# MLP of a hybrid decoder layer: first matrix in quarters 2 to 4 as seven half products a block, accumulations by ScalarE and adding transfers

## The chip, the cores and the metric

The kernel runs on one core of a Trainium2 chip. The metric is the device time of one execution in microseconds (us). Engines are named as the profile names them: PE is TensorE, PEld its weight loads, DVE is VectorE, ACT is ScalarE, POOL is GpSimd, SP is the engine whose queue starts most transfers. PSUM is the memory that PE writes to: here it is eight banks of 512 float32 columns on 128 partitions. All matrices are float32. The kernel keeps each operand as a high part rounded to PE's fp32r format and a low part that holds the rest, and makes a product from three matmuls (high by high, high by low, low by high).

## The reference

A decoder layer of 512 tokens and width 1024: two mixing branches and an output projection, then the MLP, then a gated embedding and a final norm. The change lies in the MLP:

```python
u = rmsnorm(x, norm_mlp_g[i]) @ w_up[i]              # 512 x 1024 by 1024 x 4096
x = x + jnp.square(jax.nn.relu(u)) @ w_down[i]       # 512 x 4096 by 4096 x 1024
```

The row factor of the norm commutes with the rest: relu(r a) squared is r squared times relu(a) squared. So the kernel applies only the gain ahead of the first matrix, and multiplies by the squared row factor (`r2`) when the products of the second matrix are added to x.

## The kernel before, in words

The MLP works through the 4096 hidden features in four quarters of 1024 (`for q in range(4)` near the end of `block_kernel`): `up(q)` computes a quarter's features with the first matrix, `down(q)` multiplies them by the second matrix and adds to `xk`, four tiles of 128 tokens by 1024 columns.

The input of the first matrix, `x1`, is held turned: eight tiles of 128 channels by 512 tokens, in two parts. `up` (L1239) makes eight tiles of 128 features, each a chain (`mm_T`) of 8 x 3 matmuls with the weights stationary and 512 tokens moving, into one of two banks (`ps_g`). ACT takes relu and square (L1248, L1252) into a feature tile `F`. The first two of quarter 1 are made ahead by `begin_up` (L1188), between the transposes of x1.

`down` (L1269) uses the Strassen-Winograd scheme: the two operands are cut into 2 x 2 blocks, and seven products of half size on sums and differences of blocks (named A11, A12, A22 for a block itself, S1 to S4 for sums) take the place of eight. Each product is two halves of the contraction (`kh`), two halves of the tokens (`t`) and 2 x 3 matmuls with 512 moving columns: 7 x 24 = 168 matmuls a quarter. The feature sums are made by DVE in `F` (L1262 to L1265) and split into two parts, the weight sums by DVE in place in the loaded tiles (L1302, L1306, L1320, L1326). Products accumulate in three pairs of banks X, Y, Z. `acc` (L1286) has DVE scale each half by `r2` and add it to `xk`, twelve times a quarter. The first product is part of all four output blocks: it is copied or added to a tile `p1` in each quarter, and after the last quarter scaled and added to the three blocks that don't hold it already, by six adding transfers that POOL starts (`acc_p1`, L1293).

Each weight tile of 128 x 1024 is loaded by SP into a raw tile (`wr`, four slots, or `wd`, six slots), and split by `load_w` (L156) into `wh` (ACT cast, L137) and `wl` (DVE subtraction, L138). There are four buffers of each (`WB`, L30), so splits run a few products ahead of PE and no further.

The framework sorts each engine's instructions into one fixed order when the program is built, by readiness and by their place in the text, and adds the semaphore waits. At run time each engine takes its own list in order; an instruction that waits holds those behind it. SP's loads and POOL's transfers are such lists too.

## Time and profile before

| | us |
|---|---|
| median of three runs | 870.41 (870.24 to 871.0) |
| the profiled execution | 870.98 |
| its span, first to last instruction | 869.0 |
| PE, DVE, ACT, POOL busy in the span | 859.4, 664.2, 496.6, 51.0 |

The span is what the profile covers; the time of the same execution is 1.98 us longer. A profile row gives the line of the kernel, the engine, the operation, what it writes and reads with shapes, the count, the busy time, the mean duration in ns of one, and the engine's idle time ahead with what ended it. Matmuls overlap each other, so the mean of one matmul is longer than the step from one to the next; the chain of waits and its counts give the step.

### The profile page before, as it was taken

To read this page: it belongs to the slowest core of one execution; us is meant where nothing else is said; L and a number is where in the kernel's file an instruction comes from. 1 tells how busy PE (TensorE), PEld (TensorE's weight loads), DVE (VectorE), ACT (ScalarE), POOL (GpSimd) and SP (SyncE) were. 2 spreads that over 40 slices of the span, in tenths; PEclk is the share of its full clock that TensorE was granted. 3 is DMA by queue.
4 is the path that set the end of the run, shared out by engine and by line. 5 is a ranking of instruction groups with operands and counts; after the bars stand their busy time and mean duration, and the time that the engine had idled before them with its cause. 6 is when DMAs were issued, how large, how long until landed. Compare 5 with 4: busy or idle time off the path is not lost.

```text
span 869.0 us, 11746 instructions
## 1 busy us (share of the span) xinstructions
PE 859.4 (99%) x4422; PEld 725.1 (83%) x4422; DVE 664.2 (76%) x978; ACT 496.6 (57%) x845; POOL 51.0 (6%) x81
## 2 busy tenths in 40 slices
PE   9999999999999999999999999999999999999996
PEld 7888789999877868888888888888888888888886
DVE  6898978774698898767896669746965795688657
ACT  6776657554676677854344565345535533564743
POOL 2221111000000000000020000000000000002000
PEclk9999999999999999999999999999999999999999
DMA  8677235436121256565244611630252044206502
GB/s 282 212 184 294 93 126 195 165 127 218 50 97 47 76 197 244 194 250 181 74 74 145 242 49 49 202 113 25 82 209 97 1 146 170 73 25 137 178 1 97
DMA packets 36234, 117.76 MB, mean 136 GB/s; under 512 B 5069, under 2 KB 5069, under 8 KB 36178
## 3 DMA queue, kind: packets, MB, share of 16 engines
q1 hardware_dynamic: 28578, 95.77, 31.6%
q0 software_dynamic: 7456, 20.98, 8.8%
q8 instruction: 34, 0.56, 0.3%
q10 hardware_dynamic: 144, 0.26, 0.1%
q14 instruction: 22, 0.18, 0.1%
HBM read 99.17 MB, written 11.54 MB: 127 GB/s over the span
## 4 chain that ended last, share of the span: by engine, by line
PE 86%; issue 7%; DVE 3%; ACT 2%; DMA 1%; SPq 0%; POOL 0%; POOLq 0%; ACTq 0%; DVEq 0%
PE psg L176 44%; PE psp L176 23%; PE psa L176 10%; PE pst L176 4%; PE psp L1121 1%; DMA xt<-in_x 1%; PE pst L853 1%; PE psa L783 1%; PE psa L784 1%; ACT wh L137 0%; DVE wl L138 0%; ACT lm L808 0%; DMA wh<-in_w_b 0%; PE psa L933 0%; PE psa L953 0%
## 5 line engine op out<-in xcount | busy, mean ns | idle before, releaser
L137 ACT CAST wh<-wr 128x1024 fp32r<-128x1024 f32 x129 | 135.8, 1053 | 157.0 <-PE psg L176 60.8
L138 DVE TENSOR_TENSOR wl<-wr,wh 128x1024 fp32r<-128x1024 f32 x129 | 157.2, 1220 | 81.8 <-ACT wh L137 81.5
L176 PE MATMUL psg<-x,wh 128*128 128x512 f32 x512 | 157.7, 389 | 0.0
L176 PE MATMUL psp<-wh,uf 128*128 128x512 f32 x448 | 138.5, 389 | 0.0
L176 PEld LDWEIGHTS psg<-x,wh 128*128 128x128 f32 x512 | 96.0, 188 | 20.0
L176 PE MATMUL psg<-x,wl 128*128 128x512 f32 x256 | 99.6, 389 | 0.0
L176 PEld LDWEIGHTS psp<-wh,uf 128*128 128x128 f32 x448 | 84.1, 188 | 17.4
L176 PE MATMUL psp<-wl,uf 128*128 128x512 f32 x224 | 87.1, 389 | 0.0
L176 PE MATMUL psg<-h,wh 128*128 128x512 f32 x256 | 80.1, 393 | 0.0
L137 ACT CAST wh<-wd 128x1024 fp32r<-128x1024 f32 x44 | 46.2, 1053 | 54.1 <-PE psp L176 21.9
L138 DVE TENSOR_TENSOR wl<-wd,wh 128x1024 fp32r<-128x1024 f32 x44 | 53.2, 1220 | 14.6 <-ACT wh L137 14.5
L176 PEld LDWEIGHTS psg<-x,wl 128*128 128x128 f32 x256 | 48.0, 188 | 9.9
L176 PEld LDWEIGHTS psg<-h,wh 128*128 128x128 f32 x256 | 46.9, 188 | 8.8
L176 PE MATMUL psg<-h,wl 128*128 128x512 f32 x128 | 50.0, 391 | 0.0
L138 DVE TENSOR_TENSOR uf<-F,uf 128x1792 fp32r<-128x1792 f32 (+2 forms) x20 | 33.0, 1652 | 21.8 <-ACT uf L137 21.8
L176 PEld LDWEIGHTS psp<-wl,uf 128*128 128x128 f32 x224 | 42.0, 188 | 8.9
L176 PE MATMUL psg<-yb,wh 128*128 128x512 f32 x128 | 40.1, 393 | 0.0
L1289 DVE SCALAR_TENSOR_TENSOR xk<-psp,r,xk 128x512 f32<-128x512 f32 x48 | 33.8, 745 | 8.0 <-PE psp L176 7.7
L137 ACT CAST uf<-F 128x1792 fp32r<-128x1792 f32 (+2 forms) x20 | 27.9, 1396 | 20.6 <-DVE F L1265 20.4
L176 PE MATMUL psg<-ya,wh 128*128 128x512 f32 x112 | 34.9, 391 | 0.0
L808 ACT ACTIVATE lm<-lm,nmx 128x128 f32<-128x128 f32 x64 | 25.0, 393 | 13.6 <-DVE nmx L801 13.5
L176 PEld LDWEIGHTS psg<-h,wl 128*128 128x128 f32 x128 | 24.0, 188 | 5.8 <-issue 0.8
(372 smaller groups left out, 1859.2 us busy)
## 6 DMA issues: line engine op xcount, KB each, us to landing
wr<-in_w_up SPq DMA_DIRECT2D x32, 512.0 KB, 3.2
wd<-in_w_down SPq DMA_DIRECT2D x24, 512.0 KB, 3.4
wr<-in_w_qsw SPq DMA_DIRECT2D x8, 512.0 KB, 4.1
gd<-gr POOLq DMA_DIRECT2D x8, 512.0 KB, 3.5
wr<-in_w_qkml SPq DMA_DIRECT2D x8, 512.0 KB, 3.1
wr<-in_w_b SPq DMA_DIRECT2D x8, 512.0 KB, 3.3
wh<-in_w_b POOLq DMA_DIRECT2D x8, 512.0 KB, 4.1
gl<-gd SPq DMA_DIRECT2D x8, 512.0 KB, 3.9
```

Source lines behind the costliest of these rows:

```text
L137: A.copy(dst[0], src)
L138: last_low[0] = V.tensor_sub(dst[1], src, r32(dst[0]))
L176: last_mm[0] = T.matmul(ps, l, r, start=first and i == 0, stop=last and i == len(ops) - 1, skip_group_check=parts)
L783: T.matmul(o, q[:, n * P : (n + 1) * P], kk[kp][ab][:, k0 : k0 + 256], start=True, stop=False)
L784: T.matmul(o, q[:, n * P : (n + 1) * P], kl[kp][ab][:, k0 : k0 + 256], start=False, stop=True)
L808: A.activation(lm3[:, g, :], lm3[:, g, :], AF.Exp, bias=nmx[:, g : g + 1], scale=0.125, accum_out=sm[:, g : g + 1])
L853: T.matmul(o[HALF[ab], :], v[:, c : c + 64], w[:, ab * 512 : (ab + 1) * 512], start=j == 0, stop=j == len(terms) - 1)
L1121: T.transpose(ps[:, c, m * P : (m + 1) * P], xk[m][:, (k + c) * P : (k + c + 1) * P], ident)
L1289: V.scalar_tensor_tensor(o, ps[:, t, :], r2[:, 2 * toks + t : 2 * toks + t + 1], o, ALU.mult, ALU.add)
```

## The change

Quarter 1 of the first matrix stays as eight chains, now gathered in two sets of 512 features (`up_first`). In quarters 2 to 4 the first matrix is computed by the seven-product scheme too: `up_set` makes 512 features, 2 x 256, from 512 tokens, 2 x 256, and 1024 channels, 2 x 512. Each product is 2 x 4 x 3 matmuls with 256 moving columns, into the first 256 columns of a pair's two banks; two sets make a quarter. Four weight tiles are loaded for a set and seven are split, after four sums in place. Between products the chain's pair is copied (`keep`) where a later result needs the partial sum, and three of four results are completed by a DVE add of such a copy.

The block sums of x1 are made once, in quarter 1 (`x1_sums`, and `x1_last_sum` when the quarter's chains have read the block that it overwrites); x1's tiles are wider for that, and half of them lie in new space.

In `down`, the first product accumulates in two banks of its own (`G1_`) over all four quarters and is added to all four blocks by eight adding transfers in quarter 4. Other accumulations are now an ACT scaling into a 128 x 512 tile (`kt`, four slots, shared with the copies of `up_set`) and an adding transfer that POOL starts; the last three of quarter 4 stay on DVE. The order of products changes: S2 and S3 now follow each other on the same pair. `wd` has four slots instead of six, the features of a quarter are two tiles of 7 x 512 instead of four of 7 x 256, and the space for the descriptors of POOL's transfers is set to 8192.

```diff
-    _, x1 = big_hl("x1")
+    x1b = [t.rearrange("p k c -> p (k c)") for t in big_hl("x1")[0]]
+    X1 = [[t[:, j * 1792 : (j + 1) * 1792] for t in x1b] for j in range(2)]
+    def x1_of(k):
+        return [t[:, k % 2 * 512 : (k % 2 + 1) * 512] for t in X1[k // 2]]
...
-    begun = begin_up()
...
+    X1 += [[np_.tile([P, 1792], F32R, tag="x1", bufs=4, name=nm("x1")) for _ in range(2)] for _ in range(2)]
+    x1 = [x1_of(k) for k in range(KT)]
+    begun = begin_up()
+    def F():
+        return mp.tile([P, 4, 2, 256], F32, tag="F", bufs=1, name=nm("F"))
+    def kt(n):
+        return np_.tile([P, 512], F32, tag="kt", bufs=4, name=nm(n))
+    def wd():
+        return np_.tile([P, 1024], F32, tag="wd", bufs=4, name=nm("wd"))
+    A11, A22, A12, S3, S2, S1, S4 = range(7)
...
+    def sums(s21, s11, s22, s12, s4=None):
+        V.tensor_add(s22, s21, s22)
+        V.tensor_sub(s21, s11, s21)
+        V.tensor_sub(s11, s22, s11)
+        V.tensor_sub(s12 if s4 is None else s4, s12, s11)
+    x1_s4 = []
+    def x1_sums():
+        s4 = wd()
+        for j in range(4):
+            t = wd()
+            hi, lo = [r32(q[:, :1024]) for q in X1[j]]
+            V.tensor_add(t, hi, lo)
+            x1_s4.append(s4[:, j * 256 : (j + 1) * 256])
+            sums(*[t[:, i * 256 : (i + 1) * 256] for i in range(4)], x1_s4[j])
+            split([q[:, 1024:] for q in X1[j]], t[:, :768])
+    def x1_last_sum():
+        for j in range(4):
+            split([q[:, :256] for q in X1[j]], x1_s4[j])
+    def x1_block(j, b):
+        o = {S4: 0, A11: 1, A22: 2, A12: 3, S3: 4, S2: 5, S1: 6}[b] * 256
+        return [q[:, o : o + 256] for q in X1[j]]
...
+    def own_parts(hl, fs, b, n=1):
+        o = {A11: 1, A22: 2, A12: 3}[b]
+        split([t[:, b * 512 : (b + n) * 512] for t in hl], flat(fs[:, o : o + n]))
+    def sum_parts(hl, fs):
+        sums(*[flat(fs[:, i : i + 1]) for i in range(4)])
+        split([t[:, 3 * 512 :] for t in hl], flat(fs))
...
+            if f % 4 == 0:
+                fs, hl = F(), new_uf()
...
+                    x1_sums()
+            if f % 4 == 2:
+                own_parts(hl, fs, A11)
+            if f % 4 == 3:
+                own_parts(hl, fs, A22, 2)
+                sum_parts(hl, fs)
+        x1_last_sum()
...
+    role = [pair() for _ in range(3)]
+    def up_set(i, uf):
+        X, Y, Z = role
+        role[:] = [Y, Z, X]
+        new = wr if i % 2 == 0 else wd
+        b11, b21, b12, b22 = [load_raw_to(new(), w_upb[4 * i - 8 + n]) for n in (0, 2, 1, 3)]
+        fs, hl = F(), new_uf()
+        uf.append(hl)
+        def form(raw):
+            return load_w(None, 1024, 4, raw)
+        def half(ps):
+            return ps[:, :, :256]
+        def two(t):
+            return t.rearrange("p (a b) -> p a b", a=2)
+        def prod(ps, b, w, first, last):
+            for t in range(2):
+                ops = []
+                for j in range(4):
+                    ops += pairs([h[:, j, t * P : (t + 1) * P] for h in w], x1_block(j, b))
+                chain(half(ps)[:, t, :], ops, first, last, True)
+        def keep(ps):
+            k = kt("k")
+            A.copy(two(k), half(ps))
+            return k
+        def result(slot, ps, k=None):
+            if k is None:
+                k = kt("rt")
+                A.activation(two(k), half(ps), AF.Relu)
+            else:
+                V.tensor_add(two(k), half(ps), two(k))
+                A.activation(k, k, AF.Relu)
+            A.activation(flat(fs[:, slot : slot + 1]), k, AF.Square)
+        prod(X, A11, form(b11), True, False)
+        V.tensor_sub(b12, b22, b12)
+        V.tensor_add(b11, b12, b11)
+        p1 = keep(X)
+        prod(Y, A12, form(b21), True, True)
+        result(1, Y, p1)
+        own_parts(hl, fs, A11)
+        prod(X, S2, form(b11), False, False)
+        V.tensor_sub(b21, b21, b11)
+        V.tensor_sub(b11, b22, b11)
+        u2 = keep(X)
+        prod(Z, S1, form(b11), True, False)
+        p5 = keep(Z)
+        prod(X, S3, form(b12), False, False)
+        result(2, X, p5)
+        own_parts(hl, fs, A22)
+        prod(Z, S4, form(b22), False, True)
+        result(3, Z, u2)
+        own_parts(hl, fs, A12)
+        prod(X, A22, form(b21), False, True)
+        result(0, X)
+        sum_parts(hl, fs)
...
+        new = [wr, wr, wd, wd]
+        b11, b21, b12, b22 = [
+            [load_raw_to(new[i](), w_down[q * 8 + 4 * kh + (0, 2, 1, 3)[i]]) for kh in range(2)] for i in range(4)
+        ]
+        if q == 0:
+            G1_.extend([ps_g(), ps_g()])
+        X, Y, Z = role
+        G1_p = G1_
...
+        def acc(ps, toks, n, late=False):
             for t in range(2):
-                o = xk[2 * toks + t][:, n * 512 : (n + 1) * 512]
-                V.scalar_tensor_tensor(o, ps[:, t, :], r2[:, 2 * toks + t : 2 * toks + t + 1], o, ALU.mult, ALU.add)
-        scaled = {}
-        def acc_p1(toks, n):
-            for t in range(2):
-                m = 2 * toks + t
-                if m not in scaled:
-                    scaled[m] = scratch[0].tile([P, 512], F32, name=nm("p1s"))
-                    A.activation(scaled[m], p1[:, t, :], AF.Copy, scale=r2[:, m : m + 1])
-                nc.gpsimd.dma_start(out=xk[m][:, n * 512 : (n + 1) * 512], in_=scaled[m], accum_op=ALU.add)
+                o, f = target(toks, n, t)
+                if late:
+                    V.scalar_tensor_tensor(o, ps[:, t, :], f, o, ALU.mult, ALU.add)
+                else:
+                    k = kt("ac")
+                    A.activation(k, ps[:, t, :], AF.Copy, scale=f)
+                    nc.gpsimd.dma_start(out=o, in_=k, accum_op=ALU.add)
+        def acc_p1():
+            for toks in range(2):
+                for t in range(2):
+                    k = kt("ac")
+                    A.activation(k, G1_p[t], AF.Copy, scale=target(toks, 0, t)[1])
+                    for n in range(2):
+                        nc.gpsimd.dma_start(out=target(toks, n, t)[0], in_=k, accum_op=ALU.add)
+        for kh in range(2):
+            prod(G1_p, A11, form(b11[kh]), kh, q == 0, q == 3)
         for kh in range(2):
             V.tensor_sub(b12[kh], b22[kh], b12[kh])
+            V.tensor_add(b11[kh], b12[kh], b11[kh])
         for kh in range(2):
-            w = form(b11[kh])
-            prod(X, A11, w, kh, True, False)
-            V.tensor_add(b11[kh], b12[kh], b11[kh])
-            w = form(b11[kh])
-            prod(Y, S2, w, kh, True, False)
-        if q == 0:
-            A.copy(p1, X)
-        else:
-            V.tensor_add(p1, X, p1)
+            prod(X, A12, form(b21[kh]), kh, True, True)
+        acc(X, 1, 0)
+        if q == 3:
+            acc_p1()
+        for kh in range(2):
+            prod(Y, S2, form(b11[kh]), kh, True, False)
+            V.tensor_sub(b21[kh], b21[kh], b11[kh])
+            V.tensor_sub(b11[kh], b22[kh], b11[kh])
         acc(Y, 1, 1)
-        if q == 3:
-            for toks, n in ((0, 1), (0, 0), (1, 1)):
-                acc_p1(toks, n)
-        for kh in range(2):
-            w = form(b21[kh])
-            prod(X, A12, w, kh, False, True)
-            V.tensor_sub(b21[kh], b21[kh], b11[kh])
-        acc(X, 1, 0)
         for kh in range(2):
             prod(Y, S3, form(b12[kh]), kh, False, False)
         acc(Y, 0, 1)
         for kh in range(2):
-            V.tensor_sub(b11[kh], b22[kh], b11[kh])
             prod(Z, S1, form(b11[kh]), kh, True, False)
-        acc(Z, 0, 1)
+        acc(Z, 0, 1, q == 3)
         for kh in range(2):
             prod(Y, A22, form(b21[kh]), kh, False, True)
-        acc(Y, 0, 0)
+        acc(Y, 0, 0, q == 3)
         for kh in range(2):
             prod(Z, S4, form(b22[kh]), kh, False, True)
-        acc(Z, 1, 1)
+        acc(Z, 1, 1, q == 3)
...
+        if q == 0:
+            up_first(uf)
+        else:
+            up_set(2 * q, uf)
+            up_set(2 * q + 1, uf)
...
+def _by_set(w):
+    return w.reshape(4, 2, P, 3, 2, 2, 2, P).transpose(3, 4, 1, 6, 2, 0, 5, 7).reshape(24, P, 1024)
...
-    nc = _bacc.Bacc("TRN2", target_bir_lowering=False, num_devices=1)
+    nc = _bacc.Bacc("TRN2", target_bir_lowering=False, num_devices=1, dynamic_dma_scratch_size=8192)
```

More of the change, by code (lines that the diff above doesn't have):

```diff
@@ new lines, in prod, with target @@
+                chain(ps[t] if ps is G1_p else ps[:, t, :], ops, first and kh == 0, last and kh == 1, True)
+        def target(toks, n, t):
+            return xk[2 * toks + t][:, n * 512 : (n + 1) * 512], r2[:, 2 * toks + t : 2 * toks + t + 1]
+        def acc(ps, toks, n, late=False):
+            for t in range(2):
+                o, f = target(toks, n, t)
[5 more added lines that the diff above has]
+                    nc.gpsimd.dma_start(out=o, in_=k, accum_op=ALU.add)
```

84 lines of the change are left out of this document (31 added, 53 removed).

## The prediction

> **What bounds the kernel now.** I read the page's engine totals first, then the chain of waits, then busy time by stretch of the MLP. The totals:
>
> ```profile
> span 869.0 us, 11746 instructions
> PE 859.4 (99%) x4422; PEld 725.1 (83%) x4422; DVE 664.2 (76%) x978; ACT 496.6 (57%) x845; POOL 51.0 (6%) x81
> ```
>
> TensorE (PE) is busy for 99% of the span. The chain, in order of time, shows the MLP as alternating first-matrix (psg) and second-matrix (psp) stretches:
>
> ```profile
> 136.59 2.88 PE psa L176 x24
> ...
> 484.58 40.83 PE psg L176 x180
> 525.41 38.08 PE psp L176 x168
> 563.49 43.52 PE psg L176 x192
> 607.01 38.08 PE psp L176 x168
> ...
> 726.69 43.52 PE psg L176 x192
> 770.21 38.13 PE psp L176 x168
> ```
>
> Each piece starts where the one before ends, and nothing but matmuls is on the path. The rates: 43.52 / 192 = 226.7 ns for a matmul with 512 moving columns. The first row is a chain of an earlier stage with 256 moving columns: 2.88 / 24 = 120.0 ns. Its shape is this one:
>
> ```profile
> L176 PE MATMUL psa<-h,wh 128*128 128x256 f32 x103 | 18.8, 283 | 0.0
> L176 PEld LDWEIGHTS psa<-h,wh 128*128 128x128 f32 x104 | 16.2, 192 | 0.0
> ```
>
> That is the change's shape: weights stationary, 256 tokens moving, one weight load for each matmul. The load's 192 ns is longer than the 120 ns pitch and is hidden all the same. What has slack is seen by stretch (columns: stretch, length, busy us of PE, PEld, DVE, ACT, POOL, clock, DMA):
>
> ```profile
> 484.60:525.40 40.80, 40.80 (x181) 33.76 (x181) 27.77 (x39) 26.05 (x35) 0.00 (x0) 1.00 0.31 113
> 525.40:563.50 38.10, 38.10 (x170) 31.55 (x169) 32.15 (x34) 18.58 (x19) 0.00 (x0) 1.00 0.41 139
> 563.50:607.00 43.50, 43.50 (x193) 36.02 (x193) 25.31 (x29) 21.58 (x26) 0.00 (x0) 1.00 0.21 73
> 607.00:645.10 38.10, 38.10 (x170) 31.55 (x169) 33.09 (x35) 17.50 (x18) 0.00 (x0) 1.00 0.40 138
> ```
>
> PE is at 100% in each, with the clock at 1.00. VectorE (DVE) is at 58% in a first-matrix quarter and 87% in a second-matrix quarter, ScalarE (ACT) at 50% and 46%.
>
> **TensorE's part.** In quarters 2 to 4 the first matrix took 8 chains of 24 matmuls, 512 wide: 43.52 us. Now each quarter has two sets of seven products, each 2 x 12 matmuls 256 wide: 7 x 2.88 = 20.16 us a set, 40.32 a quarter. Saved: 3.20 us a quarter, 9.60 us in three. Quarter 1 and the second matrix keep their matmul counts (180 and 168 in the rows). If PE stays as solid as now, the profiled execution's 870.98 us becomes 861.4.
>
> The Trainium skill, "TensorE: Matmul & The Clock Gate", section "Back-to-back issue gap", gives columns / 2.4 + 2.5 ns, so 109.2 and 215.8 ns; by it a set takes 18.3 us against 20.7, six sets save 14.2 us and the execution takes 856.8. This trace does not agree: 120.0 and 226.7 ns, about 11 ns more for each matmul, which is why halving the columns saves less than half.
>
> **VectorE's part, the disputed one.** The rows of the MLP window:
>
> ```profile
> L138 DVE TENSOR_TENSOR wl<-wd,wh 128x1024 fp32r<-128x1024 f32 x44 | 53.2, 1220 | 14.6 <-ACT wh L137 14.5
> L1306 DVE TENSOR_TENSOR wd<-wd,wd 128x1024 f32<-128x1024 f32 x8 | 9.7, 1218 | 0.0
> L1289 DVE SCALAR_TENSOR_TENSOR xk<-psp,r,xk 128x512 f32<-128x512 f32 x47 | 33.1, 745 | 8.0 <-PE psp L176 7.7
> L1264 DVE TENSOR_TENSOR F<-F 128x256 f32<-128x256 f32 x16 | 6.8, 425 | 0.5
> L138 DVE TENSOR_TENSOR uf<-F,uf 128x768 fp32r<-128x768 f32 x4 | 3.8, 959 | 0.0
> L138 DVE TENSOR_TENSOR uf<-F,uf 128x1792 fp32r<-128x1792 f32 x12 | 24.3, 2026 | 21.8 <-ACT uf L137 21.8
> ```
>
> From 256 and 768 columns, 1.04 ns a column: 512 columns are 0.69 us, 2048 are 2.29. A set asks of DVE seven weight splits (8.54), four sums of weight blocks (4.88), three adds from PSUM (at most 0.745 each, 2.24), three own-part splits (2.08), four feature sums (2.77) and the split of the sums (2.29): 22.80 us in 22 instructions. Back to back, instructions overlap:
>
> ```profile
> 776.69 1.22 DVE L1320 TENSOR_TENSOR wd<-wd,wd 128x1024 f32<-128x1024 f32 x1
> 777.83 1.22 DVE L138 TENSOR_TENSOR wl<-wr,wh 128x1024 fp32r<-128x1024 f32 x1
> 778.96 1.22 DVE L1312 TENSOR_TENSOR p<-psp,p 128x1024 f32<-128x1024 f32 x1
> ```
>
> They start 1.13 us apart, 0.09 under the duration, so the set costs DVE 22.80 - 22 x 0.09 = 20.8 us at best. Against 20.16 us of PE that is 103 to 113%: within a set DVE is the longer engine. The second-matrix quarter pays it back. There the twelve accumulations (12 x 0.745 = 8.9 us) and the add into p1 leave DVE, and 14 splits and 8 sums remain: 22 x 1.22 = 26.8 us of 38.1. For a whole quarter DVE has 2 x 22.8 + 26.8 = 72.4 us (66.5 at 1.13 us pitch) for 40.3 + 38.1 = 78.4 us of PE: 92 or 85%, where the rows above give (25.31 + 33.09) / 81.6 = 72%.
>
> So the question is whether DVE can work ahead. There are four split-weight buffers: while PE reads one, three may stand ready, 3 x 2.88 = 8.6 us, and the sums of weight blocks can be made earlier still, since the raw tiles' slots (four wr, four wd) are freed well before they are needed again. The excess of two sets is 1.3 to 5.3 us, less than 8.6. I therefore take no loss from the load itself; if the cover is gone, the loss is the whole excess (first rival).
>
> **The handovers in a set.** A set's chains share three bank pairs. Product 3 writes the pair that product 1 left, once ACT has copied it, and has 2.88 us for that; likewise products 5, 6 and 7. The ACT rows:
>
> ```profile
> L137 ACT CAST wh<-wd 128x1024 fp32r<-128x1024 f32 x44 | 46.2, 1053 | 54.1 <-PE psp L176 21.9 <-PE psg L176 16.3 <-DVE wd L1326 13.2
> L137 ACT CAST uf<-F 128x1792 fp32r<-128x1792 f32 x12 | 20.4, 1697 | 18.8 <-DVE F L1265 18.8
> L1252 ACT ACTIVATE F<-rt 128x512 f32<-128x512 f32 x32 | 20.3, 634 | 7.4 <-DVE uf L138 6.8
> L1248 ACT ACTIVATE rt<-psg 128x512 f32<-128x512 f32 x32 | 18.8, 588 | 1.2 <-PE psg L176 1.2
> L1298 ACT ACTIVATE p1s<-p,r 128x512 f32<-128x512 f32 x4 | 2.6, 713 | 0.0
> ```
>
> A set asks of ACT seven casts (7.37), three copies and four relus (7 x 0.588 = 4.12), four squares (2.54) and the feature casts (some 3.8, scaled by columns): 17.8 us of 20.16. A copy behind the longest cast (some 1.9 us) starts 1.9 late and ends at 2.5: in time, barely. What fails more easily is a cast at the head of ACT's queue that waits for DVE (13.2 us over four waits in the row above, 3.3 each): it holds the copy behind it, and PE waits some 1 us. A second place is the end of a set: relu, square, four sums, cast and split, 1.22 + 2.77 + 1.91 + 2.29 = 8.2 us, run while the next set's product 4, due 8.64 us in, needs its weight sum, cast and split (3.5 us) from the same engines. If the tail goes first, that split ends near 9.4, 0.8 us late. Together between 0 and 6 us over six sets; I take 0.5, because the lead of three splits covers the usual case.
>
> **The moved accumulations.** In quarters 1 to 3 ACT scales twelve half products per quarter (12 x 0.713 = 8.6 us; with 14 casts 23.3 of 38.1) and POOL issues as many adding transfers.
>
> ```profile
> L1299 POOL DMA_DIRECT2D xk<-p1s x6 | 5.2, 1601 | 331.3 <-DVE pT L138 331.3
> xk<-p1s POOLq DMA_DIRECT2D x6, 256.0 KB, 5.5
> ```
>
> Six go out in 5.2 us, 0.87 each, and land after 5.5. Four buffers, each held some 7.1 us, against two wanted every 5.44 us: enough. The tight spot is that S3 now follows S2 on the same banks: per bank ACT has the other bank's chain, 6 x 226.7 ns = 1.36 us, for 0.71 us of copy. Cost between 0 and 0.6 us a quarter, taken as 0. In quarter 4 eight more transfers of the first product use the same four buffers; if they go out in written order, S2's scalings wait for transfers to land and S3, due 16.3 us in, starts near 20.2: 3.9 us. If the first product, ready at 5.4 us, goes ahead, next to nothing. I take 1.0.
>
> **The sums of x1.** Four times an add of 1024, four of 256 and a split of 768: 4 x (1.22 + 1.70 + 0.96) = 15.5 us of DVE in quarter 1, with a last split of 1.7. The stretch has 40.8 - 27.8 = 13.0 us free; the rest goes into the next one, which has lost its accumulations. Three splits ahead cover 3 x 5.44 = 16.3 us there. Cost 0 to 2 us; I take 0.5.
>
> **The sum.** 870.98 - 9.60 + 0.5 + 1.0 + 0.5 = 863.4 us for the profiled execution. The median of the runs, 870.41, lies 0.57 below that execution, so 862.8 for a median; I give 863.0.
>
> **The rivals.**
>
> *DVE becomes the bound.* No work carries over between stages, each set takes DVE's 22.8 us, and six sets take 136.8 us where the 24 chains took 130.6: 6.2 us slower, 876.6 as a median. It decides from 21.76 us per set (130.6 / 6), where the gain is gone. For it: 103 to 113% within a set, and splits that wait for a cast (14.5 us on the wl row, 21.8 on the uf row). Against: the lead of 8.6 us, and 85 to 92% over the quarter. 0.15.
>
> *Handover waits.* PE stays the bound but loses 4 to 8 us to the copies, the tails and quarter 4's transfers: with 6 us, 867.4, as a median 866.8. For it: handovers are 2.88 us where a first-matrix chain now leaves 5.44. Against: no stall in the MLP of the present kernel. 0.27.
>
> *The 256-wide chains don't pay.* With weights from four-way interleaved tiles and x1 in new places they might cost more than 21.76 / 7 = 3.11 us per 24; then nothing is gained: 870.4. Against: the 2.88 row has the same shape. 0.05.
>
> *The other way*, the page's matmul times: 856.2 as a median. The rows speak against it. 0.03.
>
> **How the numbers follow.** The forecast, PE nearly solid with 0 to 4 us lost, has 0.50; its own range is 860.8 to 864.8. With the handover rival it reaches to about 869, and the third rival to 870.5. Range: 860.5 to 870.5, leaving out DVE as the bound and the page's times, 0.18 in all. Within 0.2% (1.7 us, about what a measurement of this kernel can tell from no change) I count the third rival and the edge of the first, 0.07; slower 0.14; faster 0.79.
>
> **What would show it.** Right: chain pieces of 2.88 us per 24 in quarters 2 to 4, about 20.2 to 21 us from set to set, second-matrix quarters still 38.1 with DVE near 27 busy, DVE above 95% in the set stretches. Wrong: set stretches of 22 us or more with PE waiting for wl (DVE the bound), gaps before products 3, 5, 6 or 7 waiting for a copy (handovers), or a gap of some microseconds before S3 in quarter 4 with ACT waiting for a buffer that a transfer holds.

## The result, and the profile after

The changed kernel takes 912.23 us (median of four runs, 909.64 to 913.14), the kernel before 870.7 on the same chip: a ratio of 1.0472 [1.0449, 1.0495]. The prediction said 863.0, at most 870.5. It had the wrong sign.

The page's totals and two of its queue lines, after. PE is busy for 95% of the span instead of 99%. Queue q0 holds the transfers that POOL starts, the adding ones among them; before, it took 8.8% of the DMA engines, with 20.98 MB.

```profile
span 911.3 us, 12851 instructions
PE 863.7 (95%) x4854; PEld 743.2 (82%) x4854; DVE 704.0 (77%) x998; ACT 550.3 (60%) x939; POOL 88.3 (10%) x125
...
q1 hardware_dynamic: 28578, 95.77, 29.7%
q0 software_dynamic: 13792, 32.52, 15.7%
```

The MLP by stretches, from the first matmul of each quarter's first and second matrix (columns as in the prediction):

```profile
485.30:528.50 43.20, 41.72 (x184) 34.00 (x183) 31.47 (x52) 28.44 (x43) 0.00 (x0) 1.00 0.28 96
528.50:571.90 43.40, 40.39 (x169) 32.30 (x168) 33.66 (x32) 25.16 (x31) 8.53 (x10) 0.96 0.61 161
571.90:616.80 44.90, 41.05 (x338) 40.45 (x337) 38.79 (x40) 30.12 (x42) 1.72 (x2) 1.00 0.38 115
616.80:656.60 39.80, 38.67 (x170) 31.37 (x169) 29.36 (x27) 24.59 (x30) 8.56 (x10) 1.00 0.62 161
656.60:701.90 45.30, 41.12 (x338) 40.50 (x337) 38.70 (x40) 30.15 (x42) 1.72 (x2) 1.00 0.39 115
701.90:741.80 39.90, 38.69 (x171) 31.39 (x170) 29.45 (x27) 24.85 (x30) 8.56 (x10) 1.00 0.63 164
741.80:787.80 46.00, 42.53 (x337) 41.92 (x336) 38.11 (x39) 30.04 (x40) 1.72 (x2) 0.96 0.37 111
787.80:850.50 62.70, 43.80 (x170) 34.28 (x169) 33.11 (x32) 24.96 (x30) 14.30 (x18) 0.84 0.55 130
```

They sum to 365.2 us, against 323.8 before: 41.4 of the span's 42.3. With PE solid (busy without a gap, at full clock) they would take 40.8 + 4 x 38.1 + 3 x 40.32 = 314.2, so 51.0 us are lost: 37.2 with PE idle (365.2 less the PE column's 328.0), and 13.8 in which PE counts as busy beyond the solid times, 10.2 of them in the three stretches whose clock is below 1.00 (42.53, 40.39 and 43.80 less 40.32 and twice 38.1). By stretch the losses are 2.4 (quarter 1's chains), 5.3 (its second matrix), 4.6, 5.0 and 5.7 (the sets), 1.7 and 1.8 (second matrix, quarters 2 and 3) and 24.6 (last quarter). What PE waited for over the MLP (total, times, longest):

```profile
PE psp L177 <- ACT wh L138: 11.8, 3, 11.1
PE psp L177 <- ACT ac L1415: 10.0, 4, 6.6
PE psp L177 <- ACT k L1346: 7.2, 5, 2.3
PE psp L177 <- DVE wl L139: 5.4, 4, 1.9
```

Two long waits stand in the last quarter; none of the others is over 2.3 us.

**How a set waits.** The change put twelve adding transfers into a second-matrix quarter, in which the next sets' weights are loaded too. The row of 28 us up to the first set, with ten of the twelve, and the DMA issues (median us from issue to landing in the last column; the last line is of the kernel before):

```profile
549.00:577.00 28.00, 25.49 (x126) 21.50 (x126) 16.24 (x15) 14.27 (x18) 8.55 (x10) 1.00 0.95 243
...
wd<-in_w_upb SPq DMA_DIRECT2D x12, 512.0 KB, 6.1
wr<-in_w_upb SPq DMA_DIRECT2D x12, 512.0 KB, 6.5
...
wr<-in_w_up SPq DMA_DIRECT2D x32, 512.0 KB, 3.2
```

The DMA engines are 95% busy, and a load of the same size lands after 6.1 to 6.5 us instead of 3.2. Now DVE's list at the first set (start, duration, engine and line; what it waited for in brackets):

```profile
566.05 1.23 DVE L1359 TENSOR_TENSOR wr<-wr,wr 128x1024 f32<-128x1024 f32 x1 [5.29 <-DMA wr<-in_w_upb]
...
574.09 1.22 DVE L1359 TENSOR_TENSOR wd<-wd,wd 128x1024 f32<-128x1024 f32 x1 [3.29 <-DMA wd<-in_w_upb]
575.23 2.35 DVE L139 TENSOR_TENSOR wl<-wr,wh 128x1024 fp32r<-128x1024 f32 x2
577.50 1.22 DVE L1366 TENSOR_TENSOR wr<-wr,wr 128x1024 f32<-128x1024 f32 x1
578.76 1.22 DVE L1367 TENSOR_TENSOR wr<-wr,wr 128x1024 f32<-128x1024 f32 x1
```

L1359 on `wd` is the *second* set's weight sum. It stands ahead of the first set's splits and sums (L139, L1366, L1367) in the fixed order, and waits 3.29 us for its load. L1367 makes the fourth product's weights; ACT's cast of them heads ACT's list and waits 6.7 us. Behind it in the list stands the copy `keep` of the *first* product, and the third product, which goes on in the first one's banks, can't start before that copy:

```profile
580.07 1.04 ACT L138 CAST wh<-wr 128x1024 fp32r<-128x1024 f32 x1 [6.70 <-DVE wr L1367]
581.02 0.58 ACT L1346 COPY k<-psp 128x512 f32<-128x512 f32 x1
...
581.65 0.51 PE L177 MATMUL psp<-x,wh 128*128 128x256 f32 x2 [2.26 <-ACT k L1346]
```

A late load that nobody yet needs has thus stopped PE, four steps on.

**The last quarter.** The gated embedding's input `p` is loaded by `ple_rows` ahead of `down(3)`. The kernel before has a tile of its own for it, `p_in`, and its load goes out early in the last quarter; PE waits nowhere in that MLP:

```profile
776.80 0.33 SPq L1341 DMA_DIRECT2D p_in<-in_p  x1
```

The change puts `p` into a `wr` slot instead, which its description above doesn't say. Its split writes into new space where the feature tile `F` was, so it waits for the last set's tail, and the last weight load of the MLP waits for the split:

```profile
800.32 1.04 ACT L138 CAST pT<-wr 128x1024 fp32r<-128x1024 f32 x1 [2.36 <-DVE uf L139]
801.40 1.23 DVE L139 TENSOR_TENSOR pT<-wr,pT 128x1024 fp32r<-128x1024 f32 x1 [1.11 <-ACT pT L138]
802.65 0.33 SPq L1269 DMA_DIRECT2D wr<-in_w_down  x1
806.19 2.94 ACT L138 CAST wh<-wr 128x1024 fp32r<-128x1024 f32 x3 [4.82 <-DMA wr<-in_w_down]
807.28 0.79 PE L177 MATMUL psp<-wh,uf 128*128 128x512 f32 x1 [11.13 <-ACT wh L138]
...
816.09 7.28 POOL L1424 DMA_DIRECT2D xk<-ac  x8
827.70 0.69 ACT L1415 ACTIVATE ac<-psp,r 128x512 f32<-128x512 f32 x1 [3.99 <-DMA xk<-ac]
828.44 0.80 PE L177 MATMUL psp<-wh,uf 128*128 128x512 f32 x1 [6.65 <-ACT ac L1415]
```

The second wait is the one the prediction described for this quarter: S2's scalings need `kt` slots that eight transfers of the first product hold.

**After some waits PE runs at half pace.** The stretches behind the two long waits, and behind one of 1.88 us in quarter 1's second matrix:

```profile
807.00:810.00 3.00, 2.56 (x5) 1.84 (x6) 2.74 (x3) 3.00 (x4) 0.00 (x0) 0.50 0.00 0
...
828.00:834.00 6.00, 5.56 (x15) 4.43 (x16) 1.23 (x1) 1.77 (x3) 0.85 (x1) 0.59 1.10 274
...
539.22 0.72 PE L177 MATMUL psp<-wl,uf 128*128 128x512 f32 x1 [1.88 <-DVE wl L139]
539.40:542.70 3.30, 3.30 (x8) 2.56 (x9) 3.30 (x5) 1.27 (x2) 0.00 (x0) 0.50 0.00 0
```

The granted clock is 0.50, 0.59 and 0.50. A wait of 2.25 us in the last sets is followed by half pace too (0.50 from 751.0 to 754.3 us), while the wait of 2.26 us in the first set leaves its row at 1.00. The Trainium skill, "TensorE: Matmul & The Clock Gate", section "What's actually happening", has PE fall to half rate after at least one idle window of some 3.4 us. The trace agrees only in part: the waits of 11.13 and 6.65 us bring it about, but so do 1.88 and 2.25 us, which are shorter than the window. In this kernel the length of a wait alone doesn't tell whether half pace follows.

### The profile page after: what moved, and what is told of

Its sections match the earlier page's. It is cut to its first block, busy times and chain, and to the rows that moved or that the text cites. A ratio compares the mean times of both kernels' runs of the same rounds, so it can differ in the third digit from the quotient of the medians.

```text
span 911.3 us, 12851 instructions
## 1 busy us (share of the span) xinstructions
PE 863.7 (95%) x4854; PEld 743.2 (82%) x4854; DVE 704.0 (77%) x998; ACT 550.3 (60%) x939; POOL 88.3 (10%) x125
## 3 DMA queue, kind: packets, MB, share of 16 engines
q1 hardware_dynamic: 28578, 95.77, 29.7%
q0 software_dynamic: 13792, 32.52, 15.7%
## 4 chain that ended last, share of the span: by engine, by line
PE 59%; DVE 15%; issue 10%; DMA 8%; ACT 5%; POOL 1%; DVEq 0%; ACTq 0%; POOLq 0%
PE psg L177 26%; PE psp L177 16%; PE psa L177 9%; DVE wl L139 5%; PE pst L177 4%; DMA wr<-in_w_upb 2%; DMA xk<-ac 2%; DMA wd<-in_w_upb 2%; ACT wh L138 2%; DVE uf L139 2%; DMA wd<-in_w_down 1%; PE psp L1122 1%; DMA wr<-in_w_down 1%; PE pst L854 1%; DVE k L1354 1%
## 5 line engine op out<-in xcount | busy, mean ns | idle before, releaser
L139 DVE TENSOR_TENSOR wl<-wr,wh 128x1024 fp32r<-128x1024 f32 x154 | 187.0, 1221 | 85.9 <-ACT wh L138 85.4
L138 ACT CAST wh<-wr 128x1024 fp32r<-128x1024 f32 x154 | 161.0, 1051 | 150.0 <-PE psg L177 40.3
L177 PE MATMUL psp<-wh,uf 128*128 128x512 f32 x384 | 125.6, 405 | 22.4 <-ACT wh L138 11.8
L177 PE MATMUL psp<-x,wh 128*128 128x256 f32 x672 | 123.4, 286 | 8.3 <-ACT k L1346 7.2
L177 PEld LDWEIGHTS psp<-x,wh 128*128 128x128 f32 x672 | 106.1, 194 | 9.8 <-ACT k L1346 8.2
L177 PE MATMUL psp<-x,wl 128*128 128x256 f32 x336 | 96.1, 286 | 3.2 <-DVE wl L139 3.1
L1416 POOL DMA_DIRECT2D xk<-ac x42 | 35.9, 947 | 344.3 <-ACT ac L1415 314.1
L177 PEld LDWEIGHTS psp<-x,wl 128*128 128x128 f32 x336 | 65.1, 194 | 3.8 <-DVE wl L139 3.8
L139 DVE TENSOR_TENSOR wl<-wd,wh 128x1024 fp32r<-128x1024 f32 x37 | 45.1, 1219 | 6.4 <-ACT wh L138 5.9
L138 ACT CAST wh<-wd 128x1024 fp32r<-128x1024 f32 x37 | 38.8, 1050 | 14.7 <-PE psp L177 14.5
L1415 ACT ACTIVATE ac<-psp,r 128x512 f32<-128x512 f32 x42 | 26.7, 685 | 31.3 <-PE psp L177 25.1
L177 PE MATMUL psg<-x,wh 128*128 128x512 f32 x128 | 39.5, 390 | 0.0
L139 DVE TENSOR_TENSOR uf<-F,uf 128x512 fp32r<-128x512 f32 (+2 forms) x30 | 34.5, 1150 | 5.4 <-ACT uf L138 5.4
L138 ACT CAST uf<-F 128x512 fp32r<-128x512 f32 (+2 forms) x30 | 29.7, 990 | 8.4 <-DVE F L1244 7.9
```

The costliest lines, as they stand in the source:

```text
L138: A.copy(dst[0], src)
L139: last_low[0] = V.tensor_sub(dst[1], src, r32(dst[0]))
L177: last_mm[0] = T.matmul(ps, l, r, start=first and i == 0, stop=last and i == len(ops) - 1, skip_group_check=parts)
L1415: A.activation(k, ps[:, t, :], AF.Copy, scale=f)
L1416: nc.gpsimd.dma_start(out=o, in_=k, accum_op=ALU.add)
```

## The experiments

All times in us; each ratio is to the kernel before, run on the same chip. Stages in order: first matrix (up) and second matrix (down) of quarters 1 to 4, from the starts of their matmuls.

| kernel | median | up1 | down1 | up2 | down2 | up3 | down3 | up4 | down4 |
|---|---|---|---|---|---|---|---|---|---|
| before | 870.7 | 40.9 | 38.1 | 43.5 | 38.1 | 43.5 | 38.1 | 43.5 | 38.1 |
| changed | 912.23 | 43.2 | 43.3 | 44.9 | 39.8 | 45.3 | 39.9 | 46.0 | 62.7 |
| rows later | 901.73 | 43.2 | 43.4 | 45.3 | 39.9 | 45.5 | 40.0 | 46.3 | 50.7 |
| thin adds | 892.17 | 43.2 | 43.4 | 40.3 | 40.3 | 40.3 | 40.0 | 40.3 | 56.1 |
| sum order | 898.77 | 43.2 | 43.1 | 41.8 | 39.8 | 41.0 | 40.0 | 42.7 | 61.7 |
| DVE acc | 899.65 | 43.2 | 48.4 | 40.3 | 41.4 | 40.3 | 43.6 | 40.7 | 52.9 |
| slots | 902.4 | 43.2 | 43.1 | 41.3 | 40.2 | 45.1 | 40.0 | 48.7 | 51.9 |
| spread | 912.98 | 40.9 | 48.7 | 42.9 | 40.1 | 45.4 | 40.2 | 46.2 | 62.5 |
| mended | 883.04 | 40.9 | 48.0 | 40.3 | 39.2 | 40.3 | 39.6 | 40.3 | 45.9 |
| mended, DVE | 887.7 | 40.9 | 47.9 | 40.3 | 40.5 | 40.4 | 40.7 | 41.6 | 48.1 |
| no x1 sums | 904.57 | 40.9 | 40.6 | 44.2 | 39.8 | 45.2 | 40.4 | 44.4 | 61.5 |
| chains | 910.13 | 40.9 | 40.6 | 45.6 | 42.3 | 45.6 | 40.7 | 45.6 | 60.8 |
| own p1 tiles | 884.26 | 40.9 | 45.0 | 40.3 | 39.5 | 40.3 | 39.6 | 42.0 | 51.3 |
| GpSimd sums | 896.69 | 52.9 | 44.2 | 40.9 | 39.7 | 40.3 | 39.6 | 40.3 | 51.2 |
| last quarter | 891.68 | 43.2 | 43.1 | 46.0 | 39.8 | 46.1 | 40.3 | 46.5 | 40.3 |
| all | 869.51 | 40.9 | 39.5 | 41.6 | 39.6 | 40.3 | 39.1 | 40.3 | 40.7 |
| all, half DVE | 874.68 | 40.9 | 41.9 | 40.8 | 40.6 | 40.3 | 40.5 | 40.9 | 41.0 |
| all, chains | 883.65 | 40.9 | 38.4 | 45.6 | 38.8 | 45.6 | 38.7 | 45.6 | 42.8 |

### Rows later: p's raw tile out of the ring

```diff
-            pT = ple_rows()
         down(q, uf)
+    pT = ple_rows()
```

> The changed kernel with one edit: the rows of p are loaded and split after the last second-matrix quarter instead of ahead of it, so that their raw tile holds no wr slot while that quarter waits for its weights. Theory A (weights come late: here because p's raw tile keeps a slot until its split can be written, at 802.6 us of the changed kernel's profile): the wait of 11.1 us and most of the slow clock behind it go, the last second-matrix quarter falls from 62.7 to about 46 us, the time from 912 to about 896 us. Theory B (VectorE has too much work in the sets): within 2 us of 912.

Measured: 901.73, ratio 1.035 [1.0335, 1.0365]; down4 falls from 62.7 to 50.7, the other stages stay within 0.4. One load in a weight slot cost 12 us of the last quarter, in one wait and the half pace behind it. More is left than the 46 us expected: the wait for S2's scalings stays, at 7.4 us.

### Thin adds: transfers of 8 KB for 256 KB

```diff
-                    nc.gpsimd.dma_start(out=o, in_=k, accum_op=ALU.add)
+                    nc.gpsimd.dma_start(out=o[:, :16], in_=k[:, :16], accum_op=ALU.add)
...
```

The eight of `acc_p1` likewise.

> The changed kernel with every adding transfer cut from 512 to 16 columns (so the sums in x are incomplete); the ScalarE scalings, the issues by GpSimd, the buffers and the order stay. Theory A (the adding transfers fill the DMA engines, loads land after 6.3 us instead of 3.2, and the sets wait for weights): loads of the first matrix's sets land after 3.2 to 4 us, the pairs of sets fall from 45.4 to 41 to 43 us, the last quarter loses its wait for the transfer buffers (6.7 us), in all 10 to 22 us faster than the changed kernel: 890 to 902. Theory B (VectorE): within 2 us of 912, but for the 6.7.

Measured: 892.17, ratio 1.024 [1.0224, 1.0256], and all three set quarters at 40.3. The same stretch ahead of the sets, a set quarter, the issues and q0's share in this kernel:

```profile
549.00:577.00 28.00, 26.87 (x135) 22.62 (x135) 20.03 (x19) 15.63 (x21) 8.58 (x10) 1.00 0.53 154
572.70:613.00 40.30, 40.30 (x337) 40.27 (x336) 35.38 (x37) 30.15 (x40) 1.72 (x2) 1.00 0.33 106
...
wr<-in_w_upb SPq DMA_DIRECT2D x12, 512.0 KB, 4.6
...
q0 software_dynamic: 13792, 19.82, 9.0%
```

POOL's column is the same to 0.03 us, and so is the number of packets; only bytes went. The DMA share falls from 0.95 to 0.53, the loads land at 4.6, and PE is solid at 40.30 of 40.30. So the sets lose their 15.3 us to the bytes of the adding transfers in the DMA engines, not to POOL's issuing and not to DVE's load, which is unchanged. (Thin transfers also give back the `kt` slots sooner; the chain of waits above goes through a load and not through such a slot.) The price follows: q0's time falls from 15.7% of 911.3 us to 9.0% of this run's 890.9, 62.9 us over 50 transfers, or 1.26 us of all sixteen engines for the bytes of each. The whole transfer costs more: from the kernel before (8.8% of 869.0 us) to the changed one, 44 more of them add 66.6 us, 1.5 each. A 512 KB load takes some 1.5 too (q1's 29.7% of 911.3 us over 95.77 MB).

### Sum order: the second set's sum behind the first set's fourth product

`issue_after` puts what stands inside it behind the named instruction in its engine's order.

```diff
-        V.tensor_sub(b12, b22, b12)
+        with tc.issue_after(fourth[0].ins) if i % 2 else ExitStack():
+            V.tensor_sub(b12, b22, b12)
...
```

> The changed kernel with one order set: in the second set of each quarter the first sum of weight blocks stands on VectorE's list behind the fourth weight split of the first set, so VectorE does not wait for the second set's load ahead of the first set's splits. Theory A: the first sets lose the waits of 3.3, 3.6 and 2.1 us, and the ScalarE cast that holds back the copy of product 1; 1.5 to 3 us a quarter, 5 to 9 us in all: 903 to 907. Theory B (VectorE's work): no change, since its work is the same, within 2 us of 912.

Measured: 898.77, ratio 1.0322 [1.0307, 1.0337]; the set quarters fall from 44.9, 45.3, 46.0 to 41.8, 41.0, 42.7. Bytes are untouched, and 10.7 of the 15.3 us come back. That is more than the 5 to 9 us expected. So most of the loss needs both: loads that are late, and a place in DVE's order where a late load holds up work for an earlier product.

### DVE acc: all accumulations back on DVE

```diff
-                if late:
+                if True:
```

> The changed kernel with all accumulations back on VectorE (twelve a quarter of 0.745 us from PSUM); only the eight adding transfers of the first product in the last quarter stay. Theory A (transfers delay the loads, and copies hold S3 back): faster than the changed kernel by 5 to 15 us, 897 to 907. Theory B (VectorE is the bound): 8.9 us more of VectorE work in each quarter, slower than the changed kernel by 5 us or more, 917 to 940.

Measured: 899.65, ratio 1.0337 [1.031, 1.0363]. Without twelve transfers a quarter the sets are solid, as with thin adds, on a row with 37.11 us of DVE work:

```profile
575.80:616.10 40.30, 40.30 (x338) 40.30 (x337) 37.11 (x40) 29.49 (x39) 0.00 (x0) 1.00 0.31 105
```

Second-matrix stages grow instead (48.4, 41.4, 43.6). Moving the accumulations off DVE does buy time there; it was paid for in the sets.

### Slots: the four raw tiles alternate between the rings

```diff
-        new = [wr, wr, wd, wd]
+        new = [wr, wd, wr, wd]
```

> The changed kernel with one edit: in the second-matrix quarters the weight blocks b11 and b12, whose last splits come first, take the wr slots, and b21 and b22 the wd slots, so that the next quarter's first set can load into wr some 5 us earlier. Theory A, as the thin transfers showed it (the sets themselves need 40.3 us a pair; the rest is weights that land late because the adding transfers share the DMA engines): the pairs of sets fall from 45.4 to 41 to 43 us, the time from 912 to 900 to 906. Rival C (it is the order on VectorE alone, and earlier loads do not matter): pairs stay within 1 us of 45.4.

Measured: 902.4, ratio 1.0358 [1.0341, 1.0376]. The time is as expected, the sets are a miss: the first pair fell to 41.3, the second stayed at 45.1 and the third rose to 48.7. The gain came in down4 (51.9), and not from `p`: PE still waits 9.07 us there for the weights behind it (11.13 in the changed kernel). The other long wait is down from 6.65 to 0.95 us, because the first product's eight transfers now go out from 801.84 us on, during the wait behind `p`.

### Spread and no x1 sums

Spread makes x1's four sums one by one, after features 2 to 5:

```diff
+            if 2 <= f < 6:
+                with tc.issue_after(done.ins):
+                    x1_sum(f - 2)
...
```

> The changed kernel with one edit: the block sums of x1 are made one tile at a time behind the features of blocks 3 to 6 of quarter 1 instead of all behind block 3. Theory D (the 15.5 us of VectorE work in one piece holds up the splits: 2.4 us lost in the first-matrix quarter, 3 more at the head of the second-matrix quarter): the two stages, 43.2 and 43.3 us now, come to 41 to 42 and 39.5 to 41, 4 to 6 us in all: 906 to 908. Rival: the work is the same and quarter 1 as a whole is full; within 1.5 us of 912.

Measured: 912.98, ratio 1.0471 [1.0446, 1.0497]. A miss: up1 is back at 40.9, but down1 rose from 43.3 to 48.7: the work was moved into the next stage, not hidden. No x1 sums leaves them out:

```diff
-            V.tensor_add(t, hi, lo)
...
+                G.memset(r32(q[:, 1024:]), 0.0)
```

> The changed kernel without the block sums of x1: GpSimd writes zeros in their place, so quarters 2 to 4 compute with wrong sums; all other instructions stay. Theory D (17 us of VectorE work for x1's sums makes quarter 1 late): the two stages of quarter 1, 43.2 and 43.3 us in the changed kernel, come to about 40.9 and 39.5 (1.3 us stays for two products on one pair of banks); 5 to 6.5 us in all: 905 to 908. Rival (the late head of the second-matrix quarter comes from the features in one tile of 2048 columns, not from x1): the second stage stays above 42.

Measured: 904.57, ratio 1.0374 [1.0352, 1.0396]. Quarter 1 is 81.5 instead of 86.6 us. Its two rows:

```profile
484.50:525.40 40.90, 40.90 (x183) 33.86 (x182) 25.53 (x32) 24.98 (x38) 0.00 (x0) 1.00 0.34 114
525.40:566.00 40.60, 39.00 (x170) 31.27 (x169) 25.86 (x24) 24.20 (x28) 8.50 (x10) 1.00 0.67 166
```

The sums cost 5.1 us, 2.3 in up1 and 2.8 in down1. Down1 keeps 2.5 us of loss without them; in 1.6 of these PE waits for a split of the features (`uf`) on DVE.

### Chains: no sets, accumulations as changed

```diff
-        if q == 0:
-            up_first(uf)
-        else:
-            up_set(2 * q, uf)
-            up_set(2 * q + 1, uf)
+        up_first(uf, q)
...
```

> The changed kernel with the sets undone: quarters 2 to 4 of the first matrix are chains of 512 columns again, without x1's sums; the accumulations by ScalarE and adding transfers, the kept banks, the order of products and the slots stay. Theory A (loads are late beside the adding transfers): a chain needs a weight tile only every 5.44 us, so the first-matrix quarters stay near 43.5, the second-matrix ones at 39.4 to 40, and the last loses 15 to 24 us by p's raw tile and the transfers' buffers; 889 to 898. Rival (the sets are what is slow): within 2% of the kernel before, below 882.

Measured: 910.13, ratio 1.0444 [1.0429, 1.046]: a miss. Without any set and without x1's sums the kernel is as slow as the changed one: the rest of the change, the moved accumulations and the last quarter, loses enough by itself, and the sets of the changed kernel, with x1's sums, gave nothing net. The 45.6 us of a first-matrix stage here, for 43.5 before, don't mean slower chains. Seven matmuls of the second matrix run inside the stage, ahead of the last chain:

```profile
604.21 0.39 PE L177 MATMUL psg<-wh,uf 128*128 128x512 f32 x1
...
605.80 0.72 PE L177 MATMUL psp<-x,wh 128*128 128x512 f32 x2
```

At 226.7 ns each they are 1.6 of the 2.1 us, and the next stage has them less.

### Last quarter: quarter 4 accumulates as before

On top of rows later, `down(3)` takes back its old order: the first product goes on into A12 on its banks, four scaled copies feed six adding transfers after S2, the rest is added by DVE.

```diff
+            for m in range(NT):
+                scaled[m] = kt("ac")
+                A.activation(scaled[m], G1_p[m % 2], AF.Copy, scale=r2[:, m : m + 1])
...
+            for toks, n in ((0, 1), (0, 0), (1, 1)):
...
```

> The changed kernel with p's rows after the last quarter and the last second-matrix quarter in the earlier way: accumulations on VectorE, the first product copied and its banks continued by the A12 product, six adding transfers, S2 ahead of A12. The other quarters stay as changed. Theory E (what the last quarter still loses without p's raw tile, 50.75 us against 38.1, is scalings that wait for buffers held by the first product's transfers, and PE at half pace after that wait): the last quarter comes to 38.5 to 40.5 us, the time to 888 to 891. Rival (VectorE's late sums of the last set hold up any last quarter): 44 us or more, above 894.

Measured: 891.68, ratio 1.0227 [1.0212, 1.0243]; down4 is 40.3 us, 10.4 below rows later. With that run's 12.0 this accounts for 22.4 of the last quarter's 24.6 us. The edit takes back quarter 4's scalings, transfers and order at once, so 10.4 is the price of these together.

```profile
790.20:830.40 40.20, 38.72 (x169) 31.14 (x169) 35.08 (x37) 20.22 (x23) 7.36 (x10) 1.00 0.54 144
```

### Mended, and mended with DVE

Rows later, sum order, slots and spread together, in quarters 1 to 3 the order A11, A12, S2, S1, S3, S4, A22 (so that S3 no longer follows S2 on the same pair), and quarter 4 on DVE but for one result:

```diff
+        if q < 3:
+            for kh in range(2):
+                prod(Z, S1, form(b11[kh]), kh, True, False)
+            acc(Z, 0, 1)
+            for kh in range(2):
+                prod(Y, S3, form(b12[kh]), kh, False, False)
...
```

> The changed kernel with five edits together: p's rows after the last quarter; the order of the sums in the second sets; the slots as in the run before; x1's sums spread; the products of the second matrix ordered so that no two neighbours share a pair of banks (quarters 1 to 3: S2, S1, S3, S4, A22), with quarter 4's accumulations on VectorE but for one and the first product's transfers issued first. Theory A with all its places (late weights by loaded DMA engines and by held slots, neighbours on one pair, x1's sums): sets near 41 a pair, second-matrix quarters near 38.5, in all 9.6 saved and 3 to 6 lost: 864 to 868, faster than the kernel before. Rival (VectorE's 92% of a quarter is too much once the other waits are gone): 872 to 885.

Measured: 883.04, ratio 1.013 [1.0114, 1.0145]: a miss, in the rival's range. The sets are solid; 9.9 us are lost in down1 (x1's sums: all, chains, which has the same order and no sums, takes 38.4 there) and 7.8 in down4. The same kernel with every accumulation on DVE (`if late:` to `if True:`):

> The run before (five edits) with the accumulations of all quarters on VectorE; only the first product's eight transfers remain. Theory A: no adding transfers beside the loads, so sets at 40.3 a pair; VectorE has 35.8 us of work in a second-matrix quarter, 74 to 81 us in a whole one of 78.4: second-matrix quarters between 38.5 and 42, in all 862 to 874. Rival (VectorE is the bound): above 880, with PE waiting for wl in every stage.

Measured: 887.7, ratio 1.0178 [1.0163, 1.0193], a miss and 4.7 slower: with the sets mended, the adding transfers pay. The rival's time came, but not its sign: PE waits 6.7 us at one place for an accumulation on DVE (`xk`) and 5.2 in all for `wl`, not in every stage.

### Own p1 tiles, and GpSimd sums

Own p1 tiles gives the first product's scaled copies two tiles of their own, and makes half of x1's sums inside `down(0)`:

```diff
-                    k = kt("ac")
+                    if not t:
+                        pair_ = scratch[0].tile([P, 1024], F32, tag="e", bufs=2, name=nm("p1s"))
+                    k = pair_[:, t * 512 : (t + 1) * 512]
...
```

> The mended kernel with two more edits in place of the spread sums: half of x1's sums are made inside the first second-matrix quarter, in the feature tile that is free then, and quarter 4 keeps the changed kernel's scalings and transfers, with the first product's copies in tiles of their own so that no scaling waits for a buffer. Theory A with D: sets 40.3 a pair, second-matrix quarters 40, 39.3, 39.6 and 40, quarter 1's chains 41: 866 to 871. Rival (VectorE's load in quarter 1 cannot be placed without a loss of 5 us or more): 873 to 880.

Measured: 884.26, ratio 1.0146 [1.0129, 1.0163]: a miss. PE waits as long as ever, for another reason:

```profile
PE psp L177 <- ACT ac L1431: 8.9, 2, 8.3
...
POOL xk L1432 <- DMA xk<-p1s: 8.2, 2, 8.0
```

POOL's next transfer adds to a block to which a transfer of the first product is still adding, so POOL waits for it to land, and with it everything behind. More buffers don't help where this kernel makes transfers to one target follow each other. GpSimd sums has GpSimd make x1's sums early:

```diff
-            V.tensor_add(t, hi, lo)
+            G.tensor_add(t, hi, lo)
...
```

> As the run before, but all of x1's sums in the first-matrix quarter with their adds on GpSimd, which has nothing to do there; VectorE keeps the splits, 17.2 - 11.7 = 5.5 us. Theory D: quarter 1's stages come to 41 and 39.5 to 40: 865 to 870. Rival (GpSimd's adds are slow or hold VectorE up, no row shows them): quarter 1 longer than 84 us, 873 or more.

Measured: 896.69, ratio 1.03 [1.0279, 1.0321]: a miss, up1 is 52.9. GpSimd's add of 128x1024 takes 2748 ns, DVE's 1216:

```profile
L1254 POOL TENSOR_TENSOR wd<-x,x 128x1024 f32<-128x1024 f32 x4 | 11.0, 2748 | 50.5 <-ACT wd L1235 50.5
```

### All: every mend that had worked

Mended's orders, the last quarter as before, and x1's sums in three places: half early, a quarter after S3 and a quarter after A22 of `down(0)`.

```diff
+            acc(Y, 0, 1)
+            if q == 0:
+                x1_late_sum(2)
...
+            acc(Y, 0, 0)
+            if q == 0:
+                x1_late_sum(3)
...
```

> All mends: p's rows late, the order of the sums, the slots, alternating pairs in quarters 1 to 3, the last quarter in the earlier way, and x1's sums one half early and one half inside the first second-matrix quarter behind the fourth and the last of its later products. If the places found are all there are: quarter 1 at 82 us for its two stages (79.0 before), sets 40.3 a pair, 39.2, 39.6 and 39.5 for the other second-matrix quarters, 9.6 saved and about 7 lost: 866 to 870, faster than the kernel before by 0.1 to 0.6%. Rival (x1's sums cost 5 to 8 us wherever they stand, as in the two tries before): 872 to 877.

Measured: 869.51, ratio 0.9981 [0.9972, 0.999]: 0.19% faster than before, which is at the edge of what can be told. The row of the one set quarter that isn't solid:

```profile
564.80:606.40 41.60, 40.82 (x338) 40.41 (x337) 37.32 (x39) 30.50 (x41) 1.94 (x3) 1.00 0.51 135
```

Its stages sum to 322.0, 1.8 under before and 7.8 over the solid 314.2. Of the scheme's 9.6 us the sets keep 8.3 (two of three quarters at 40.3); the second-matrix quarters, 158.9 us for 152.4 before, give back 6.5. Two variants say why it isn't more. Half DVE puts three more accumulations of quarters 1 to 3 on DVE:

```diff
-            acc(Z, 0, 1)
+            acc(Z, 0, 1, True)
...
```

> As the run before with half of the accumulations of quarters 1 to 3 on VectorE, so half the adding transfers and 4.5 us more VectorE work in each second-matrix quarter. If transfers are what is left of the loss: 1 to 3 us faster than the run before. If VectorE's work is: 2 to 5 us slower.

Measured: 874.68, ratio 1.0032 [1.0021, 1.0044], 5.2 slower for some 4.5 us more DVE work a quarter (6 x 0.745) and half the transfers: DVE has little room left in the second-matrix quarters, and the transfers aren't what is left of the loss. All, chains takes the sets away and, with them, x1's sums:

```diff
+        up_first(uf, q)
...
```

> The mended kernel with the sets undone: chains of 512 columns in all quarters, no sums of x1; transfers, kept banks and all other mends stay. It gives what the sets are worth when nothing else is in their way: by the matmul counts 9.6 us, less what x1's sums cost in quarter 1. Expected: first-matrix quarters 43.5, second-matrix quarters 39 to 40, 873 to 877; if the sets bring nothing even then, within 2 us of the mended kernel.

Measured: 883.65, ratio 1.0146 [1.0132, 1.016]: a miss, 14.1 us slower than with sets. The sets are worth having. Again some of the second matrix, six matmuls or 1.36 us, runs inside each first-matrix stage of the chains; counted where they belong, the first matrix is 10.5 us slower in the profiled executions and the second 3.9.

## Why the prediction was wrong

Against 2.0 us of losses in the prediction's sum, the changed kernel lost 51.0. By size: the last quarter 24.6, the sets 15.3, quarter 1 7.7, the second matrix of quarters 2 and 3 3.5. Two steps carry most of it: the cover for late weights in the sets, and the price of quarter 4, from which a load was missing.

*The saving on TensorE* was right: 40.3 us a quarter where nothing is late (thin adds, DVE acc, all), 9.6 saved. The rivals about dear 256-wide chains and about faster matmuls are out.

*DVE as the bound* was rightly refused for the sets: they run solid with 35.4 to 37.1 us of DVE work. The work of a whole quarter, 66.5 to 72.4 us, was right as well: 38.79 + 29.36 = 68.2 in quarter 2. Half DVE shows how little is left over.

*The step of the argument that failed* is the cover: "the raw tiles' slots (four wr, four wd) are freed well before they are needed again", and with them the lead of three splits. It took for granted that loads land as before, in 3.2 us. The transfers were priced by POOL's issue and by the time they hold buffers, never by the DMA engines they share with the loads: ten at 1.26 to 1.5 us are 12.6 to 15 of 28 us, the loads land at 6.1 to 6.5, and the lead is gone. Thin adds showed this cause; sum order showed that the fixed order on DVE turns most of it into a stall. Together 15.3 us in the sets, where the sum has nothing for late weights.

*The handovers* had the right mechanism, a cast at the head of ACT's queue that holds the copy behind it. 7.2 us over five waits, up to 2.3 each (part of the 15.3), against 0.5 taken and 6 as the bound. But what set them off was the late load, not the tail of a set: with thin adds none is left.

*S3 after S2 on one pair* was taken at 0, at most 0.6 a quarter. The trace has a wait of 1.13 us before S3 in each of quarters 1 to 3, 3.4 us in all. In quarter 2:

```profile
633.61 1.26 ACT L1415 ACTIVATE ac<-psp,r 128x512 f32<-128x512 f32 x2 [1.91 <-PE psp L177]
634.93 0.50 PE L177 MATMUL psp<-wh,uf 128*128 128x512 f32 x1 [1.13 <-ACT ac L1415]
```

ACT had nothing to do for 1.91 us before the two scalings, and still the first started only with the end of S2, when the whole pair was done; so the other bank's chain covered nothing.

*Quarter 4* was taken at 1.0 with 3.9 as the bound. The mechanism was right, but this part measured 10.4 (rows later to last quarter): a wait of 6.65 us, 7.4 in rows later, and half pace behind it. The larger part, 12.0, isn't in the sum at all: the new place of `p`'s raw tile, in the MLP's ring, was never priced.

*The sums of x1* were taken at 0.5, at most 2; they cost 5.1. Spread showed that they don't disappear into the next stage as argued: that stage has no 16 us of cover.

*Half pace after a wait* was in no case. The three stretches with a clock below 1.00 hold 10.2 us of PE time beyond the solid one, mostly 5.7 in the last quarter.

What stays open: 0.9 of the 2.5 us that down1 loses without x1's sums, 0.7 of the last 2.2 us of down4 (in the other 1.5, in the run last quarter, PE waits for accumulations on DVE), and why some waits of about 2 us bring half pace and others don't.

## What to carry to other kernels

Price a moved operation on every resource that it lands on: an adding transfer also takes DMA engine time from the loads that run beside it, and a lead counted in buffers is worth nothing once loads land later. For each new or moved instruction, ask what stands behind it in its engine's fixed order and which ring's slot it holds until when; a wait for something not yet needed stops PE as surely as one for something needed. When a sum relies on slack, check the next stage too: spread only moved the loss there.

## What the runs showed of the hardware

An adding transfer of 256 KB inside the chip takes some 1.3 to 1.5 us of all sixteen DMA engines, nearly as much as a 512 KB load (1.5). GpSimd's two-input add of 128x1024 took 2.26 times DVE's time (2748 and 1216 ns). Half pace followed waits of PE as short as 1.88 and 2.25 us, for some 3.4 us each time. And in a solid set PEld is busy for 40.30 of 40.30 us as well as PE: the weight loads are back to back there, which may be why 256 columns take 120 ns rather than half of 226.7; no run tested it.
